# A four-layer diffusion trunk on one core: ten planned orders for its instruction queues, wider products in the last layer, and sixteen softmax scalings on GpSimd

## The chip, the core and the metric

One core of a Trainium2 chip runs the whole program. The metric is the time on the device of one execution, in microseconds (us). The core has TensorE (PE in the rows; its weight loads stand apart as PEld), VectorE (DVE), ScalarE (ACT), GpSimd (POOL) and SyncE (SP), which issues the DMAs. Each engine works through its own queue in order, and the queues wait for each other by semaphores.

## The reference, cut to what matters

Two streams of 256 tokens by 1024 features go through four layers: the latent tokens `x` and the context tokens `ctx`. Each layer has an attention and a SwiGLU feed-forward part, both with a norm before and after. The context reads only itself, the latent stream reads both. After the last layer's keys and values the context isn't needed any more.

```python
for i in range(DEPTH):                      # mixers 0, 1, 2, 0 = A, B, C, A
    h  = rmsnorm(x, g[0]) * (1.0 + sc1) + sh1
    hc = rmsnorm(ctx, g[0]) * (1.0 + csc1) + csh1
    y, yc = attention(h, hc, ...)
    x = x + gt1 * rmsnorm(y, g[1])
    h = rmsnorm(x, g[2]) * (1.0 + sc2) + sh2
    x = x + gt2 * rmsnorm(swiglu(h, ffn_w13[i], ffn_w2[i]), g[3])
    if not last:
        ctx = ...                           # the same, with yc and its own modulation
```

All is fp32. The feed-forward part is `(silu(h @ gate) * (h @ up)) @ w2` with 2816 hidden features.

## The kernel before, in words

**Products.** Every fp32 operand of a large product is split into a high and a low part (`wh`, `wl` of a weight tile, `hh`, `hl` of an activation), and `mm3` (lines 520 to 524) issues three matmuls: high by high, high by low, low by high. Weights come in units of 512 KB: a DMA into `wr`, ACT copies it to `wh` (line 420), DVE subtracts to `wl` (line 536). A unit is 128 output features of `q`, `k`, `gate` or `up` (`feature_major`, weights stationary, 256 tokens of one stream moving), or a piece of `v`, `o`, `w2` (`token_major`, `block_unit_product`, activations stationary, 512 weight columns moving). In the first three layers `gate` and `up` of both streams go together from the third unit on: `feature_major_both` moves 512 columns, the tokens of both streams side by side. That works since `both_h[k]` holds, for feature block k, the high parts of the context and the latent tokens and then the low parts of both, in one tile of four times 256 columns.

**Attention.** For each head, `scores` are matmuls, DVE takes the maximum (or adds bias or mask and takes it in one step), ACT takes the exponential with its sum, the rows are scaled by the reciprocal sum, `flip` transposes the result on TensorE, and a product with `v` follows (`att_a`, `att_bc`). In layer C (the third) the latent queries come in two tiles of 128; the first tile's 128 by 512 exponentials are scaled on DVE (line 1057), the second's on ACT, and the context's, 128 by 256 at a time, on GpSimd (line 1054). GpSimd also does half of the rotary embedding (lines 872, 873) and the two small steps of each norm (704, 706).

**Order.** Nothing is emitted where it is written. Every step is an `Op` with an engine, an assumed duration and a priority; `Plan.schedule` puts all of them in an order by list scheduling, `Plan.latest` goes back through it for latest starts, and the next round mixes both into new priorities (`ROUNDS`). The order with the shortest planned time is emitted. While it picks a step, the scheduler holds a PSUM bank that one engine touched closed to the others until that engine's step has ended (`touch`).

**Seams.** At the end of `o` and of `w2` the residual and both norms have to be gone through (`emit_kept`: ACT squares, DVE, GpSimd, DVE), then TensorE transposes the result (`prenorm_flips`, line 762), and ACT and DVE split it into the operands of the next products. The planner puts the products of one stream over the norm chain of the other.

## Time and profile before

| | |
|---|---|
| median of 3 runs | 2272.24 us (2271.04 to 2272.55) |
| the profiled execution | 2271.76 us |
| its span, first to last instruction | 2269.9 us |
| TensorE busy | 2209.3 us (97%) |
| VectorE busy | 1636.9 us (72%) |
| ScalarE busy | 1061.1 us (47%) |
| GpSimd busy | 218.7 us (10%) |
| mean granted clock of TensorE | 0.992 |

The ends of matmuls are modelled, so that matmuls which follow each other without a pause overlap in the record, and a busy TensorE isn't one at its peak. Read the distance from one start to the next instead: where it is the shortest that this form shows, TensorE is the limit; where it is longer, TensorE waited. The rows that the argument rests on have a section of their own below.

### The profile page before, as it was taken

What the parts mean: (1) busy time and instruction counts of PE and PEld (TensorE: products, weight loads), DVE (VectorE), ACT (ScalarE), POOL (GpSimd) and SP (SyncE); (2) the same over time, 40 slices, a digit from 0 to 9 for tenths busy, and PEclk for the clock granted to TensorE, in tenths of its full rate; (3) what the DMA queues carried; (4) which work ended last, traced back from release to release, by engine and by line L of the source; (5) the groups of instructions that cost most, each with busy time, mean ns of one, the idle gap of its engine ahead of it and who ended that gap; (6) DMA issues with size and microseconds to landing.
All of it is one profiled execution on the core that took longest, in us unless ns stands there. A gap on an engine that the chain in (4) does not pass through costs nothing.

```text
span 2269.9 us, 35835 instructions
## 1 busy us (share of the span) xinstructions
PE 2209.3 (97%) x13236; PEld 1926.1 (85%) x13236; DVE 1636.9 (72%) x3114; ACT 1061.1 (47%) x2245; POOL 218.7 (10%) x300
## 2 busy tenths in 40 slices
PE   7999999999999999999999999999999999998998
PEld 5889888888888998888878899888887878997997
DVE  5888699887354887878773489997877345996454
ACT  5478642223344776522233469852223333785443
POOL 0111010000011231200000032020000000311000
PEclk9999999999999999999999999999999999999999
DMA  9743266664243433566643430256664233444653
GB/s 298 221 122 117 87 200 230 213 209 159 96 121 100 114 100 112 177 206 201 195 145 107 126 93 12 84 185 194 209 193 146 102 112 94 132 119 131 185 185 140
DMA packets 369278, 338.91 MB, mean 149 GB/s; under 512 B 33120, under 2 KB 282960, under 8 KB 369104
## 3 DMA queue, kind: packets, MB, share of 16 engines
q1 hardware_dynamic: 369104, 336.63, 47.2%
q8 instruction: 104, 1.70, 0.3%
q14 instruction: 70, 0.57, 0.1%
HBM read 321.77 MB, written 1.17 MB: 142 GB/s over the span
## 4 chain that ended last, share of the span: by engine, by line
PE 84%; DVE 9%; ACT 3%; issue 2%; POOL 1%; DMA 1%; DVEq 0%; POOLq 0%; SPq 0%; ACTq 0%
PE bkl L522 19%; PE bkl L524 19%; PE bkl L523 19%; PE bkc L523 7%; PE bkc L522 7%; PE bkc L524 6%; ACT f L420 1%; DVE wl L536 1%; PE bkc L650 1%; PE bkl L935 1%; DVE r L943 1%; DVE col L923 1%; DVE r L884 1%; PE bkl L915 1%; PE bkl L762 1%
## 5 line engine op out<-in xcount | busy, mean ns | idle before, releaser
L420 ACT ACTIVATE wh<-wr 128x1024 fp32r<-128x1024 f32 x380 | 402.6, 1061 | 818.7 <-PE bkl L523 502.5
L536 DVE TENSOR_TENSOR wl<-wr,wh 128x1024 fp32r<-128x1024 f32 x380 | 469.5, 1237 | 339.8 <-ACT wh L420 338.5
L522 PE MATMUL bkl<-h,wh 128*128 128x256 f32 (+1 forms) x1872 | 637.3, 340 | 0.0
L524 PE MATMUL bkl<-h,wl 128*128 128x256 f32 (+1 forms) x1872 | 632.0, 338 | 0.0
L523 PE MATMUL bkl<-h,wh 128*128 128x256 f32 (+1 forms) x1872 | 631.9, 338 | 0.0
L643 DVE SCALAR_TENSOR_TENSOR f<-f,cs,f 128x512 f32<-128x512 f32 x556 | 386.6, 745 | 7.2 <-DMA f<-in_ada_w 6.5
L522 PEld LDWEIGHTS bkl<-h,wh 128*128 128x128 f32 x1872 | 355.5, 190 | 42.4 <-issue 4.5
L524 PEld LDWEIGHTS bkl<-h,wl 128*128 128x128 f32 x1872 | 355.3, 190 | 37.9
L523 PEld LDWEIGHTS bkl<-h,wh 128*128 128x128 f32 x1872 | 355.5, 190 | 36.9
L522 PE MATMUL bkl<-wh,h 128*128 128x512 f32 (+1 forms) x560 | 219.5, 392 | 0.0
L524 PE MATMUL bkl<-wh,h 128*128 128x512 f32 (+1 forms) x560 | 216.6, 387 | 0.0
L523 PE MATMUL bkl<-wl,h 128*128 128x512 f32 (+1 forms) x560 | 216.5, 387 | 0.0
L522 PE MATMUL bkc<-wh,h 128*128 128x512 f32 (+1 forms) x472 | 185.4, 393 | 0.0
L523 PE MATMUL bkc<-wl,h 128*128 128x512 f32 (+1 forms) x472 | 183.3, 388 | 0.5 <-DVE wl L536 0.5
L524 PE MATMUL bkc<-wh,h 128*128 128x512 f32 (+1 forms) x472 | 183.1, 388 | 0.6 <-DVE h L716 0.6
L704 POOL TENSOR_SCALAR col<-col 128x1 f32<-128x1 f32 x58 | 33.5, 578 | 1485.5 <-ACT j L420 1422.9
L523 PE MATMUL bkc<-h,wh 128*128 128x256 f32 x496 | 142.2, 287 | 2.4 <-DVE h L776 2.3
L522 PE MATMUL bkc<-h,wh 128*128 128x256 f32 x496 | 143.2, 289 | 0.8 <-ACT h L420 0.8
L524 PE MATMUL bkc<-h,wl 128*128 128x256 f32 x496 | 141.5, 285 | 0.0
L522 PEld LDWEIGHTS bkl<-wh,h 128*128 128x128 f32 x560 | 105.3, 188 | 22.0 <-issue 1.0
L524 PEld LDWEIGHTS bkl<-wh,h 128*128 128x128 f32 x560 | 105.2, 188 | 21.6
L523 PEld LDWEIGHTS bkl<-wl,h 128*128 128x128 f32 x560 | 105.3, 188 | 19.9
(215 smaller groups left out, 3395.5 us busy)
## 6 DMA issues: line engine op xcount, KB each, us to landing
wr<-in_ffn_w SPq DMA_DIRECT2D x264, 512.0 KB, 3.9
f<-in_ada_w SPq DMA_DIRECT2D x384, 256.0 KB, 4.4
wr<-in_a_wqkv SPq DMA_DIRECT2D x48, 512.0 KB, 3.8
f<-gd SPq DMA_DIRECT2D x54, 256.0 KB, 5.2
r<-r SPq DMA_DIRECT2D x96, 128.0 KB, 2.3
wr<-in_b_wqkv SPq DMA_DIRECT2D x24, 512.0 KB, 3.8
wr<-in_a_wo SPq DMA_DIRECT2D x16, 512.0 KB, 3.5
wr<-in_c_wqkv SPq DMA_DIRECT2D x12, 512.0 KB, 3.8
```

Of the source, the lines that this page charges most:

```text
L420: nc.scalar.activation(o(), i(), func, **k)
L522: nc.tensor.matmul(o, lh, rh, start=first, stop=False)
L523: nc.tensor.matmul(o, lh, rl, start=False, stop=False)
L524: nc.tensor.matmul(o, ll, rh, start=False, stop=last)
L536: dve(lambda: nc.vector.tensor_tensor(l.ap, raw.ap, f32(h.ap[:]), ALU.subtract), t_dve(1024), [raw, h], [l], p)
L643: dve(lambda b=b, raw=raw, c=c: nc.vector.scalar_tensor_tensor(b.ap, raw.ap, c(), b.ap, ALU.mult, ALU.add), t_dve(512, extra=0.06), [raw, ...
L650: nc.tensor.matmul(acc.ap[32 * j:32 * j + 32, u * 256:(u + 1) * 256], lhs, tiles[j // 2].ap[:, (j % 2) * 256:(j % 2 + 1) * 256], start=fir ...
L704: op("pool", 0.25, lambda: nc.gpsimd.tensor_scalar(r.ap[:, 1:2], ss.ap[:, 0:1], ss.ap[:, 1:2], D * EPS, ALU.add, ALU.add), [ss], [r])
L762: nc.tensor.transpose(tp.ap[:, c0:c0 + P], xn[t, k // 4].ap[:, (k % 4) * P:(k % 4 + 1) * P], ident.ap)
L884: dve(lambda r0=r0, r1=r1, m=m: nc.vector.scalar_tensor_tensor(qs.ap[r1, m, :], src()[r0], QSCALE, f32(qs.ap[r0, m, :]), ALU.mult, ALU.sub ...
L915: nc.tensor.matmul(o, q, kt()[:, 0, :], start=True, stop=False)
L923: dve(lambda: nc.vector.tensor_reduce(nm.ap[:, 0:n], b.ap[:].rearrange("p (i k) -> p i k", i=n), AX.X, ALU.max, negate=True), t_dve(512), ...
```

## The change

**The planner.** Ten rounds in place of four; each tuple now has two entries more (`hold`, `shake`; `shake` is zero in all ten). The `touch` rule goes out of the scheduler. In its place each finished order is gone through once more by a new function, `replay`, with other durations for some steps and with waits between the engines on a bank, and the order whose replayed time is the shortest is emitted. With `hold`, DVE and ACT may leave a step for a more urgent one that is ready within 0.4 of the step's duration.

**The last layer.** `k` of both streams is one product of 512 columns (`QK_BOTH = (3,)`). The latent stream's `gate` and `up` go through `feature_major_parts`: for each feature block one matmul of 512 columns with `wh` (the latent tokens' high parts and, beside them, their low parts), and one of 256 columns with `wl`. The two halves of the bank are two partial sums, and `sum_parts` adds them: ACT copies one half to SBUF, DVE adds the other. For this the latent low parts are put where the context's low parts were (`hlc`).

**GpSimd.** In layer C the first latent query tile's scaling moves from DVE's `tensor_scalar` to a GpSimd `tensor_tensor` whose second operand is the reciprocal, broadcast along the row.

```diff
-ROUNDS = [(0.0, 0.0), (0.7, 0.05), (0.7, 0.05), (0.75, 0.0)]
+ROUNDS = [(0.0, 0.0, 0.0, 0.0), (0.7, 0.05, 0.0, 0.0), (0.7, 0.05, 0.0, 0.0), (0.75, 0.05, 0.0, 0.0), (0.6, 0.05, 0.0, 0.0),
...
-QK_BOTH = False
+QK_BOTH = (3,)
+ON_POOL = {"B": [], "C": [0]}
...
-            time = max(o.end for o in order)
+            time = self.replay(order)
...
+    def replay(self, order):
+        free, end, held, users, bank = {}, {}, {}, {}, {}
+        for o in order:
...
+            t = free.get(o.eng, 0.0)
+            for x in o.deps:
+                t = max(t, end[x] + (0.0 if x.eng == o.eng else AFTER[x.eng]))
...
+        return max(end[o] for o in order)
...
-                    for b in o.bufs:
-                        if b.touch:
-                            for other, end in b.touch.items():
-                                if other != e:
-                                    t = max(t, end + LAT)
...
+                    if self.hold and e in ("dve", "act"):
+                        sooner = [x for x in can if t < x[0] < t + self.hold * o.dur and x[1] < p - URGENT]
+                        if sooner:
+                            t, p, q, o = min(sooner)
...
+                if i == DEPTH - 1 and which == 1:
+                    lb = Buf(f"hlc{k}")
...
+    def feature_major_parts(s, w, H, bank):
+        wh, wl, h3, l3 = w
+        for half in range(2):
+            def go(half=half):
+                for k in range(4 * half, 4 * half + 4):
+                    parts = both_h[k][:].rearrange("p m s t -> p (m s t)")[:, T:3 * T]
+                    wide = bank.ap[:]
+                    if k < KD - 1:
+                        nc.tensor.matmul(wide, h3()[:, k, :], parts, start=(k == 0), stop=False)
+                    nc.tensor.matmul(bank.ap[:, 0:T], l3()[:, k, :], both_h[k][:, 0, 1, :], start=False, stop=False)
+                    if k == KD - 1:
+                        nc.tensor.matmul(wide, h3()[:, k, :], parts, start=False, stop=True)
+            pe(4 * 0.325, go, [wh, wl] + [b for k in range(4 * half, 4 * half + 4) for b in H[k]], [bank], unit=True)
+
+    def sum_parts(bank):
+        x, y = Buf("f1"), Buf("f1")
+        act(lambda: x.ap, lambda: bank.ap[:, T:2 * T], AF.Copy, t_act(T), [bank], [x])
+        dve(lambda: nc.vector.tensor_tensor(y.ap, bank.ap[:, 0:T], x.ap, ALU.add), t_dve(T), [bank, x], [y])
+        return y
...
+                    elif qts[0] in ON_POOL[kind] and j >= FROM[kind]:
+                        op("pool", 1.35, lambda e=e, r=r: nc.gpsimd.tensor_tensor(
+                            e.ap, e.ap, r.ap[:, 0:1].to_broadcast([P, nk]), ALU.mult), [r], [e])
...
+            if last:
+                gate_bank = Buf("bk" + s, cap=("gu" + s, 4))
+                feature_major_parts(s, w, S.H, gate_bank)
+                boost[0] = BOOST["F"]
+                g, S.sg = sum_parts(gate_bank), Buf("f1")
+                act(lambda sg=S.sg: sg.ap, lambda: g.ap, AF.Silu, t_act(T, False), [g], [S.sg])
...
-            if both and unit[0] in "qk" and QK_BOTH:
+            if both and unit[0] in "qk" and L in QK_BOTH:
```

What the planner makes of it, at three places. Names: `bkc` and `bkl` are PSUM banks of the context and the latent stream, `h_72` to `h_79` the tiles `both_h[0]` to `both_h[7]`, `ident` the identity of a transpose, `f_...` a buffer of 128 by 512 or 128 by 256 elements. Lines 522 to 524 are 561 to 563 in the changed file, 762 is 801, 872 and 873 are 936 and 937, 1054 is 1118.

TensorE, the seam from `o` to the feed-forward part in layer A, first layer: before, the last latent products of `o` and then the transposes of the context's norm.

```order
L522 MATMUL bkl<-wh,h_79 128x512
L523 MATMUL bkl<-wl,h_79 128x512
L524 MATMUL bkl<-wh,h_79 128x512
L762 MATMUL bkc<-ident,f_3729 128x128
L762 MATMUL bkc<-ident,f_3757 128x128
```

The same seam in the changed program, between the first and the second pair of transposes.

```order
L801 MATMUL bkc<-ident,f_3685 128x128
L801 MATMUL bkc<-ident,f_3700 128x128
L561 MATMUL bkl<-wh,h_76 128x512
L562 MATMUL bkl<-wl,h_76 128x512
L563 MATMUL bkl<-wh,h_76 128x512
L561 MATMUL bkl<-wh,h_77 128x512
L562 MATMUL bkl<-wl,h_77 128x512
L563 MATMUL bkl<-wh,h_77 128x512
L561 MATMUL bkl<-wh,h_78 128x512
L562 MATMUL bkl<-wl,h_78 128x512
L563 MATMUL bkl<-wh,h_78 128x512
```

Before, all latent products stand ahead of all context transposes; now 12 latent products of 512 columns stand between the two pairs of transposes and 6 behind the second, ahead of the first context `gate`.

TensorE, the seam from the third layer to the fourth: before, from the last context product of `w2` on (18 latent products of 512 columns, lines 522 to 524 in turn, up to the two rows of transposes at the end).

```order
L524 MATMUL bkc<-wh,h_77 128x512
L522 MATMUL bkl<-wh,h_75 128x512
L523 MATMUL bkl<-wl,h_75 128x512
L524 MATMUL bkl<-wh,h_75 128x512
L522 MATMUL bkl<-wh,h_75 128x512
```

The same place in the changed program.

```order
L563 MATMUL bkc<-wh,h_77 128x512
L561 MATMUL bkl<-wh,h_74 128x512
L562 MATMUL bkl<-wl,h_74 128x512
L563 MATMUL bkl<-wh,h_74 128x512
L561 MATMUL bkl<-wh,h_74 128x512
```

Six products more, those of `h_74`, now stand behind the last context product: 24 in place of 18 ahead of the first transpose of the context's norm.

GpSimd in layer C, the middle of the heads: before, the rotary steps of the latent stream (872, 873) and the context's scalings (1054).

```order
L1054 TENSOR_TENSOR f_14208<-f_14208,col 128x256 x2
L1054 TENSOR_TENSOR f_14215<-f_14215,col 128x256 x2
L872 TENSOR_TENSOR f_14399<-f_14399,sinT 128x256
L873 TENSOR_TENSOR f_14519<-f_14519,f_14399 128x256
L1054 TENSOR_TENSOR f_14385<-f_14385,col 128x256 x2
```

In the changed program, with the latent scalings (1121) between them.

```order
L936 TENSOR_TENSOR f_14275<-f_14275,sinT 128x256
L937 TENSOR_TENSOR f_14218<-f_14218,f_14275 128x256
L1121 TENSOR_TENSOR f_14226<-f_14226,col 128x512
L1118 TENSOR_TENSOR f_14320<-f_14320,col 128x256 x2
L1118 TENSOR_TENSOR f_14331<-f_14331,col 128x256 x2
L936 TENSOR_TENSOR f_14480<-f_14480,sinT 128x256
L1121 TENSOR_TENSOR f_14270<-f_14270,col 128x512
L937 TENSOR_TENSOR f_14493<-f_14493,f_14480 128x256
```

Sixteen instructions of 128 by 512 elements stand newly in GpSimd's queue, ahead of context scalings and even between the two steps of one rotary embedding.

## Rows read from the trace of the kernel before

**Rows 1.** The page's first part: busy time of an engine, its share of the span, number of instructions.

```profile
PE 2209.3 (97%) x13236; PEld 1926.1 (85%) x13236; DVE 1636.9 (72%) x3114; ACT 1061.1 (47%) x2245; POOL 218.7 (10%) x300
```

**Rows 2.** Busy time by stretch: the stretch and its length, then for each engine the busy us and the instructions that began, then the granted clock of TensorE, the DMA share and GB/s. In turn: the end of the first layer's attention, its seam, the second layer's seam, the third layer's attention, its seam, the pause before the fourth layer, the transposes and first products after it, the fourth layer's attention, its `gate` and `up`.

```profile
170.00:293.00 123.00, 120.92 (x830) 106.96 (x829) 94.57 (x206) 86.74 (x221) 19.91 (x26) 1.00 0.37 112
293.00:304.00 11.00, 7.77 (x49) 6.81 (x49) 11.00 (x21) 8.45 (x23) 4.35 (x7) 0.84 0.49 172
...
925.00:934.00 9.00, 6.93 (x42) 6.40 (x41) 9.00 (x17) 8.15 (x19) 4.28 (x5) 0.81 0.90 289
...
1300.00:1480.00 180.00, 172.34 (x1312) 163.57 (x1311) 162.63 (x471) 146.67 (x415) 43.90 (x59) 1.00 0.23 68
1480.00:1512.00 32.00, 30.81 (x193) 27.06 (x192) 29.44 (x50) 21.84 (x51) 11.17 (x16) 1.00 0.66 208
...
1869.00:1874.00 5.00, 0.46 (x5) 0.14 (x2) 4.10 (x6) 4.63 (x13) 2.92 (x4) 0.80 0.16 38
1874.00:1882.30 8.30, 7.54 (x23) 6.09 (x24) 7.90 (x14) 3.52 (x10) 2.35 (x5) 0.50 0.37 114
...
1925.00:2060.00 135.00, 128.94 (x964) 122.33 (x963) 119.12 (x249) 97.47 (x219) 30.05 (x32) 0.99 0.45 129
...
2077.00:2206.00 129.00, 129.00 (x1065) 128.43 (x1064) 63.67 (x74) 56.68 (x76) 0.00 (x0) 1.00 0.59 176
```

**Rows 3.** The timeline of TensorE at full clock: start, duration, engine, line, operation, tiles, form. The first two rows are the first and the last of 32 matmuls of 512 columns that follow each other without a pause; the last five, from the fourth layer's start, are matmuls in a row, one of 512 columns and then four of 256.

```profile
1861.82 0.39 PE L523 MATMUL bkl<-wl,h 128*128 128x512 f32 x1
...
1868.85 0.39 PE L524 MATMUL bkl<-wh,h 128*128 128x512 f32 x1
...
1925.36 0.39 PE L524 MATMUL bkl<-wh,h 128*128 128x512 f32 x1
...
1925.58 0.28 PE L522 MATMUL bkl<-h,wh 128*128 128x256 f32 x1
...
1925.70 0.28 PE L523 MATMUL bkl<-h,wh 128*128 128x256 f32 x1
...
1925.82 0.28 PE L524 MATMUL bkl<-h,wl 128*128 128x256 f32 x1
...
1925.94 0.28 PE L522 MATMUL bkl<-h,wh 128*128 128x256 f32 x1
```

**Rows 4.** Groups of instructions of the last layer's `gate` and `up` (2076 to 2207 us): line, engine, operation, tiles, form, count, then busy us and mean ns of one, then idle time before them.

```profile
L523 PE MATMUL bkl<-h,wh 128*128 128x256 f32 x352 | 99.9, 284 | 0.0
...
L420 ACT ACTIVATE wh<-wr 128x1024 fp32r<-128x1024 f32 x45 | 47.6, 1058 | 72.7 <-PE bkl L523 72.3 <-PE bkl L524 0.3
L420 ACT ACTIVATE f<-bkl 128x256 f32<-128x256 f32 x22 | 8.1, 368 | 0.0
...
L536 DVE TENSOR_TENSOR wl<-wr,wh 128x1024 fp32r<-128x1024 f32 x45 | 55.2, 1226 | 64.9 <-ACT wh L420 64.9
L1410 DVE TENSOR_TENSOR gal<-bkl,f 128x256 f32<-128x256 f32 x16 | 6.7, 419 | 0.5 <-ACT f L420 0.5
```

**Rows 5.** The timeline of TensorE at the seams of the first, the second and the third layer; in brackets the engine's idle time before the instruction and what ended it.

```profile
297.31 0.98 PE L762 MATMUL bkc<-ident,f 128*128 128x128 f32 x7 [2.92 <-DVE f L745]
...
927.05 0.39 PE L522 MATMUL bkc<-h,wh 128*128 128x256 f32 x1 [0.78 <-ACT h L420]
...
928.72 0.38 PE L523 MATMUL bkc<-h,wh 128*128 128x256 f32 x1 [1.29 <-DVE h L776]
...
1874.00 1.97 PE L762 MATMUL bkc<-ident,f 128*128 128x128 f32 x8 [4.54 <-DVE f L745]
...
1876.72 0.90 PE L762 MATMUL bkc<-ident,f 128*128 128x128 f32 x3 [0.76 <-DVE f L745]
```

**Rows 6.** Stretches in which TensorE's granted clock stood at half, behind the idle times of rows 5 (columns as in rows 2), and the timeline of matmuls of 256 and of 512 columns inside them.

```profile
298.50:301.90 3.40, 3.36 (x15) 2.98 (x16) 3.40 (x8) 1.63 (x6) 1.01 (x3) 0.50 0.02 8
930.00:933.40 3.40, 3.40 (x18) 3.40 (x17) 3.40 (x6) 3.34 (x6) 1.25 (x1) 0.51 0.87 321
1872.10:1882.20 10.10, 7.45 (x23) 6.00 (x24) 8.80 (x16) 5.08 (x14) 4.08 (x8) 0.50 0.34 98
...
300.16 0.41 PE L522 MATMUL bkc<-h,wh 128*128 128x256 f32 x1
...
300.38 0.41 PE L523 MATMUL bkc<-h,wh 128*128 128x256 f32 x1
...
1878.70 0.63 PE L522 MATMUL bkc<-wh,h 128*128 128x512 f32 x1
...
1879.13 0.63 PE L523 MATMUL bkc<-wl,h 128*128 128x512 f32 x1
```

**Rows 7.** The third layer's attention (1300 to 1480 us): the groups of DVE's and of GpSimd's scalings; line 1054 over the whole execution (minimum, median and maximum ns of one); a GpSimd instruction that ran while DVE split a weight tile; and TensorE's waits for a transpose (`flip`, line 935) in this stage: us in total, times, longest.

```profile
L1057 DVE TENSOR_SCALAR f<-f,col 128x512 f32<-128x512 f32 x16 | 7.9, 499 | 0.1
...
L1054 POOL TENSOR_TENSOR f<-f,col 128x256 f32<-128x256 f32 x32 | 21.1, 682 | 34.0 <-ACT f L420 15.9 <-DVE col L1049 7.4 <-DVE col L1051 5.7
...
L1054 POOL TENSOR_TENSOR f<-f,col x64: 607/615/1595, 732.8 to 1395.7; 128x256 f32<-128x256 f32 x64
...
1334.35 1.22 DVE L536 TENSOR_TENSOR wl<-wr,wh 128x1024 fp32r<-128x1024 f32 x1
1334.43 1.73 POOL L873 TENSOR_TENSOR f<-f,f 128x256 f32<-128x256 f32 x1
...
PE bkl L935 <- ACT f L420: 1.6, 2, 1.4
PE bkl L935 <- DVE f L1057: 1.3, 1, 1.3
...
PE bkl L935 <- DVE col L1051: 0.9, 1, 0.9
```

More of the change, by code (lines that the diff above doesn't have):

```diff
@@ L2 @@
 import math
+import random
 from contextlib import ExitStack
@@ L58 @@
 ALONE = 2
-QK_BOTH = False
+QK_BOTH = (3,)
 LATE = 5
+ON_POOL = {"B": [], "C": [0]}
+FROM = {"B": 0, "C": 0}
+URGENT = 4.0
+SEED = 1
+NEAR = 8.0
+TRUE_PE = [(12 * 0.109, 12 * 0.120), (6 * 0.216, 6 * 0.227), (12 * 0.216, 12 * 0.227), (4 * 0.325, 4 * 0.347),
+           (0.436, 0.472), (0.872, 0.944), (0.654, 0.72), (0.66, 0.5)]
+AFTER = {"pe": 0.2, "act": 0.15, "dve": 0.12, "pool": 0.12, "dma": 0.0}
 TAIL = {"o": 0, "early o": 2, "w2": 4}
@@ L168, in run @@
         self.times = []
-        for mix, wait in ROUNDS:
+        noise = random.Random(SEED)
+        for mix, wait, self.hold, shake in ROUNDS:
             for b, c in count.items():
                 b.left = c
-                b.touch = {}
             for b in self.fixed:
@@ L177, in run @@
                 for o, (start, late) in zip(self.ops, now[1]):
-                    o.prio = (1 - mix) * start + mix * late
+                    o.prio = (1 - mix) * start + mix * late + (noise.uniform(-shake, shake) if shake else 0.0)
             try:
@@ L185, in run @@
                 continue
-            time = max(o.end for o in order)
-            self.times.append(round(time, 1))
+            time = self.replay(order)
+            self.times.append((round(max(o.end for o in order), 1), round(time, 1)))
             if best is None or time < best[0]:
                 best = time, order, [b.slot for b in self.fixed], [(o.start, o.end) for o in self.ops]
-            if now is None or time < now[0] + TOL:
+            if now is None or time < now[0] + TOL and time < best[0] + NEAR:
                 late = self.latest(order)
@@ L206, in run @@
             o.fn()
+    def replay(self, order):
+        free, end, held, users, bank = {}, {}, {}, {}, {}
+        for o in order:
+            d = o.dur
+            if o.eng == "pe":
+                d = next((b for a, b in TRUE_PE if abs(d - a) < 0.001), d)
+            elif o.eng == "pool":
+                d = {0.7: 1.0, 0.25: 0.45, 0.4: 0.6, 0.75: 0.8}.get(d, d)
+            t = free.get(o.eng, 0.0)
+            for x in o.deps:
+                t = max(t, end[x] + (0.0 if x.eng == o.eng else AFTER[x.eng]))
+            for x in o.after:
+                t = max(t, end[x, "start"])
+            for b in o.bufs:
+                if b.slot is not None and b.slot >= 0:
+                    at = self.kinds[b.kind][0], b.slot
+                    if held.get(at) is not b:
+                        users[at, 0] = users.get((at, 1), [])
+                        users[at, 1] = []
+                        held[at] = b
+                    for x in users[at, 0]:
+                        t = max(t, end[x] + (0.0 if x.eng == o.eng else AFTER[x.eng]))
+                    if b.kind[:2] == "bk":
+                        for x in users[at, 1]:
+                            if x.eng != o.eng:
+                                t = max(t, end[x] + 0.1)
+                    users[at, 1].append(o)
+            end[o, "start"] = t
+            free[o.eng] = t + d
+            end[o] = t + d + (2.5 if o.eng == "dma" else 0.0)
+        return max(end[o] for o in order)
     def latest(self, order):
@@ L314, in schedule @@
             cand[o.eng].remove(o)
-            for b in o.bufs:
-                if b.kind[:2] == "bk":
-                    b.touch[o.eng] = o.end
             for b in o.bufs:
@@ L1404, in run_unit @@
         elif nm == "up":
+            dst, at = (S.g[0], n) if n < 16 else (S.g[1], n - 16)
+            if last:
+                up_bank, sg = Buf("bk" + s, cap=("gu" + s, 4)), S.sg
+                feature_major_parts(s, w, S.H, up_bank)
+                boost[0] = BOOST["F"]
+                u = sum_parts(up_bank)
+                dve(lambda: nc.vector.tensor_tensor(dst.ap[:, at, :], u.ap, sg.ap, ALU.mult), t_dve(T), [u, sg], [(dst, at)])
+                boost[0] = 0.0
+                return
             gu, sg = S.gu, Buf("f1")
-            dst, at = (S.g[0], n) if n < 16 else (S.g[1], n - 16)
             feature_major(s, w, S.H, gu, T)
```

6 lines of the change are left out of this document (4 added, 2 removed).

## The prediction

> **What bounds the kernel now.** I read the page's busy times first: TensorE is busy 97% of the span, DVE 72%, GpSimd 10% [rows 1]. TensorE's ends are modelled, so I went to the stretches by stage and to the distances between its starts. At full clock, 31 steps between 32 matmuls of 512 columns take 7.03 us, 0.227 us each; three steps of 256 columns take 0.36 us, 0.120 us each [rows 3]. Two matmuls of 256 columns thus cost 0.240 us, one of 512 costs 0.227 us: 13 ns go with the instruction, not with its columns. By these distances TensorE runs without a gap through the last layer's `gate` and `up` [rows 2]. What it loses elsewhere, it loses in two kinds of place. At the seams between `o` and the feed-forward part, and ahead of the last layer, it stands idle for a norm chain, and behind that its granted clock is at half (1.2 in place of 2.4 GHz) for 3.4 or 10.1 us [rows 5, 6]. In the attention of the third and fourth layers it is busy 172.3 of 180 and 128.9 of 135 us, with DVE close behind at 162.6 and 119.1 us [rows 2]. So an edit pays in full if it saves TensorE's own time in the feed-forward stage, or its idle time at a seam; in attention, only as far as DVE's and GpSimd's chains let it.
>
> **The last layer's gate and up.** There are 44 units of 8 feature blocks, 352 blocks with three matmuls of 256 columns each [rows 4]. Before: 352 x 3 x 0.120 us. After: 352 x (0.227 + 0.120) us. The difference is 352 x 0.013 = 4.6 us, on TensorE's own path in a stage where nothing else ends last. No row shows the two widths in turn on the same bank; the step from 512 to 256 columns takes 0.22 us, and the next ones 0.12 us [rows 3]. The bounds: nothing, if the 13 ns come back in the mixed pair, and 9.2 us, if the weight load behind the wide matmul hides so well that the narrow one loses its 13 ns too. I take -4.6 us, since both distances are this kernel's own. What is added is hidden: 44 ACT copies of 0.37 us, 16 us more on an ACT that is busy 57 of 129 us, and 44 DVE additions of 0.42 us, 18 us more on a DVE busy 64 of 129 us [rows 2, 4]. Were that cover gone, a unit's copy and addition, 0.8 us, would hold one bank longer, and four are allowed for.
>
> The Trainium skill ("TensorE: Matmul & The Clock Gate", under "Wait — 56ns, not 53.3ns?") puts the fixed cost of a warm matmul at 2.5 ns beyond its columns. By it this edit would be worth 352 x 2.5 ns = 0.9 us. The 13 ns in the rows disagree, and the rows decide; the case stands among the rivals.
>
> **The last layer's k.** Eight units, 24 matmuls each for both streams: 192 pairs become 192 wide ones, 192 x 0.013 = 2.5 us of TensorE. The stage has DVE at 119.1 of 135 us and idle places of its own, and now the splits of both streams' keys come at once. I take -2.0 us, between 0 and -2.5.
>
> **The seams.** Four places lose idle time and, behind it, clock. I price the clock by the rows at half: 256 columns take 0.215 us there, so 3.4 us lose 3.4 x (1 - 0.120 / 0.215) = 1.5 us; 512 columns take 0.43 us, so the 8.3 us of TensorE's work between 1874.0 and 1882.3 lose 8.3 x (1 - 0.227 / 0.43) = 3.9 us [rows 2, 6].
> First layer: 2.9 us idle for the second pair of transposes, and 1.5 us of clock: 4.4 us at stake. Before, all latent products of `o` stood ahead of the context's transposes; now 12 of them, 2.7 us, stand between the two pairs and 6 behind. I take -3.5 us.
> Second layer: 0.8 + 1.3 us idle ahead of the first `gate` matmuls [rows 5] and 1.5 us of clock, 3.6 us at stake. The changed order sets the last latent products behind the transposes here as well. I take -2.5 us.
> Third layer: TensorE is busy 30.8 of 32 us [rows 2], 1.2 us at stake. I take -0.8 us.
> Ahead of the fourth layer: 4.5 + 0.8 us idle [rows 5] and 3.9 us of clock. Six more products of 0.227 us, 1.4 us, now stand behind the last context product. The idle time falls to some 3 us, and I leave the clock as it is: -1.4 us, or up to -5.3 if it no longer falls for as long.
> Together -8.2 us. The ends are 0, if the chains through ACT, DVE and GpSimd, which are reordered too, get as much longer, and -14.5 us, the whole stake. The fifth seam, in the last layer, has one stream and nothing to put over it; it stays.
>
> **The scaling on GpSimd.** DVE loses 16 x 0.499 = 8.0 us of the 162.6 us that it works in this stage. GpSimd gets 16 instructions of twice the elements of line 1054, whose median is 0.615 us: up to 16 x 1.23 = 19.7 us, beside 43.9 us of work in 180 us, so it isn't the bound by its total [rows 2, 7]. But each scaling now takes 0.73 us longer ahead of its transpose. And beside a weight split on DVE a step of the rotary embedding took 1.73 us on GpSimd, and line 1054's longest is 1.595 us against its median of 0.615 [rows 7]: about 1 us more where that happens, so 1.7 us longer. Queued behind each are the context's scalings and the rotary steps of the next heads; the latent scores wait for those, with a whole head's products in between. TensorE already waited 3.8 us in this stage for transposes that had late inputs [rows 7]. Those are four waits among 32 latent transposes of scaled tiles, so most have some cover. I take +2 us: three of the sixteen exposed at 0.73 us. The ends are -4 us, if DVE's 8.0 us shorten the waits for DVE, and +27 us, sixteen times 1.7.
>
> The Trainium skill ("GPSIMD Engine Reference", under "8. Key points") speaks against this edit: DVE is about twice as fast for elementwise work, and GpSimd shares its SBUF interfaces with DVE's instructions that read two SBUF tensors. The weight split is such an instruction, and the trace agrees with both: 0.615 us for half the elements that DVE does in 0.499 us, and 1.73 us beside a split [rows 7].
>
> **The rest of the new order** in attention: steps move by a few places on every engine, some waits get more work over them and some less. I see no sign in it: 0, plus or minus 5 us.
>
> **The sum.** -4.6 - 2.0 - 8.2 + 2.0 = -12.8 us. Against the profiled execution's 2271.76 us (span 2269.9 and 1.9 around it), that is 2259.0 us; that execution stands 0.5 us under the median of 2272.24, so the median after is 2259 us, 0.6% less.
>
> **The rivals.** A measurement of this kernel tells 0.2%, 4.5 us, from no change; the border is at 2267.7 us.
> *GpSimd becomes the late engine (slower).* Each of the sixteen transposes waits for its scaling: 16 x 1.2 us, between the free and the contended price, is 19 us in place of 2, so 2259 + 17 = 2276 us. For it: GpSimd works in order, its steps beside weight splits take a microsecond more, and six scalings stand in a row at the end of the stage. Against it: 180 us hold 64 us of GpSimd work, and few flips waited before. It decides from some 1 us of uncovered wait per flip on. 9 in 100.
> *The order gives nothing.* Where one wait goes, another engine's queue is next; the seams come out as before, and what stays are the wider products and GpSimd's price: -4.6 - 2.0 + 2.0, so 2267 us, on the border. For it: the planner's durations are assumed ones, and the new durations are in the choice alone, not in the picking. 15 in 100, half of it within 0.2%.
> *The seams give all.* The idle times go and the clock stays up, -14.5, with the products' -6.6 and nothing for GpSimd: 2251 us. 18 in 100.
> *The wide matmuls save only 2.5 ns each* (the page's rule): 0.9 + 0.5 us in place of 6.6, so 2264 us. Against it stand all the distances of rows 3. 5 in 100.
> My forecast has the other 53 in 100.
>
> **How the numbers follow.** 2259 us is the likeliest case. Its own spread is about 2252 to 2266. The range goes up to 2270, over the case without gain from the order, and down to 2247, under the case in which the seams give all; it leaves out the slower case and little else. Faster by over 0.2%: the forecast's 53, 18, 5, and about half of the 15, less a few for the spread: 78 in 100. Within 0.2%: 13. Slower: 9.
>
> **What would show it.** In the profile after: blocks of the last `gate` and `up` every 0.347 us, and the stage some 5 us shorter; idle times ahead of the context's transposes and the first `gate` under 1 us in the first two layers, with no half clock behind them; under 4 us ahead of the fourth layer. In the third layer's attention, 16 GpSimd steps of 1.2 us and more, DVE 8 us less, and waits for `flip` that name GpSimd of 2 us in all. The prediction is wrong if those waits come to over 10 us, if the seams' idle times stand elsewhere again, or if the mixed pairs of 512 and 256 columns take 0.36 us.

## The result, and the profile after

| | before | after |
|---|---|---|
| median, same chip | 2271.77 us (6 runs, 2270.07 to 2272.67) | 2259.65 us (6 runs, 2258.39 to 2261.73) |
| ratio, 95% interval | | 0.9948 [0.9935, 0.9961] |
| span of the profiled execution | 2269.9 us | 2257.8 us |
| mean granted clock of TensorE | 0.992 | 0.996 |

The changed kernel is 0.52% faster; 2259.0 us were predicted. The page's first part, busy time by engine, answers to [rows 1]:

```profile
PE 2200.0 (97%) x12692; PEld 1892.5 (84%) x12692; DVE 1649.2 (73%) x3142; ACT 1074.6 (48%) x2289; POOL 235.9 (10%) x316
```

TensorE has 544 matmuls (192 of `k`, 352 of `gate` and `up`) and 9 us less. DVE has 12 us more, which the additions bring: e9 below, without GpSimd's scaling, has 12.6 us more too (1649.5 us). That the sixteen scalings went freed next to nothing on DVE, for a reason that e3 shows.

To see where the 12 us are, I cut both traces at the same matmuls, each time at the first of a named unit. "L1" to "L3" is the context's ninth `gate` unit of the first to the third layer.

| stretch, us | before | after | difference |
|---|---|---|---|
| start to L1 | 390.12 | 386.20 | -3.9 |
| L1 to L2 | 630.13 | 630.75 | +0.6 |
| L2 to L3 (holds layer C's attention) | 568.78 | 570.67 | +1.9 |
| L3 to the fourth layer's first `q` | 336.56 | 331.76 | -4.8 |
| to its first `gate` | 149.75 | 147.69 | -2.1 |
| to its first `w2` | 127.45 | 124.42 | -3.0 |
| to the end | 67.08 | 66.34 | -0.7 |

The timeline of TensorE after, at the first layer's seam and ahead of the fourth layer, answers to [rows 5]; the stretches (columns as in rows 2) answer to [rows 2, 6]: the first and the second layer's seam, the third layer's attention, a part of it at half clock, its seam, the two parts of the pause ahead of the fourth layer, the fourth layer's attention, the half clock at its end, its `gate` and `up`.

```profile
288.82 0.39 PE L563 MATMUL bkl<-wh,h 128*128 128x512 f32 x1
289.05 1.03 PE L801 MATMUL bkc<-ident,f 128*128 128x128 f32 x8
289.84 0.48 PE L561 MATMUL bkl<-wh,h 128*128 128x512 f32 x1
...
292.67 1.03 PE L801 MATMUL bkc<-ident,f 128*128 128x128 f32 x8
293.46 0.48 PE L561 MATMUL bkl<-wh,h 128*128 128x512 f32 x1
...
294.92 0.28 PE L561 MATMUL bkc<-h,wh 128*128 128x256 f32 x1
...
1867.78 0.27 PE L801 MATMUL bkc<-ident,f 128*128 128x128 f32 x1
1870.47 1.09 PE L801 MATMUL bkc<-ident,f 128*128 128x128 f32 x8 [2.42 <-DVE f L784]
1872.33 0.55 PE L801 MATMUL bkc<-ident,f 128*128 128x128 f32 x3 [0.77 <-DVE f L784]
```

```profile
289.00:300.00 11.00, 10.94 (x75) 9.91 (x74) 10.94 (x19) 7.70 (x18) 3.17 (x5) 1.00 0.82 246
920.00:929.00 9.00, 8.89 (x60) 7.91 (x58) 8.94 (x16) 6.32 (x15) 2.52 (x4) 1.00 0.79 241
1298.00:1478.00 180.00, 172.45 (x1296) 162.81 (x1295) 161.76 (x452) 145.13 (x409) 57.72 (x74) 0.99 0.22 64
1378.30:1381.60 3.30, 3.30 (x17) 3.30 (x17) 3.30 (x14) 1.72 (x9) 0.00 (x0) 0.50 0.03 12
1478.00:1510.00 32.00, 31.25 (x198) 27.86 (x197) 27.45 (x46) 22.14 (x52) 11.97 (x16) 1.00 0.65 205
1864.00:1869.00 5.00, 4.05 (x19) 3.06 (x18) 5.00 (x7) 4.97 (x13) 1.47 (x2) 1.00 0.08 9
1869.00:1877.00 8.00, 5.63 (x29) 4.09 (x30) 7.34 (x14) 6.15 (x15) 4.29 (x7) 1.00 0.38 132
1919.00:2049.00 130.00, 123.45 (x760) 110.34 (x759) 113.27 (x248) 95.80 (x215) 29.70 (x32) 0.99 0.45 130
2069.00:2191.00 122.00, 122.00 (x694) 106.05 (x693) 75.71 (x107) 65.76 (x111) 0.00 (x0) 1.00 0.61 182
...
2057.50:2067.70 10.20, 4.19 (x18) 3.83 (x19) 8.15 (x13) 6.31 (x16) 4.29 (x6) 0.50 0.35 103
```

At the first seam the transposes now stand between products, with no idle time in brackets and the clock at 1.00; before it was 2.92 us idle and then 3.4 us at half. The second seam looks the same. Ahead of the fourth layer 2.4 + 0.8 us are idle in place of 4.5 + 0.8, and in this profile the clock stays up where it stood at half for 10.1 us. The 10.2 us at half ahead of the last `gate` (2057.5) are the fifth seam, which stayed.

In the third layer's attention the clock fell for 3.4 us (from 1378.2), where before it did not. This is what the +1.9 us of L2 to L3 are. Seven variants below run the same order; in the profiles of three of them (e1b, e8, e11) the clock stays up there, and L2 to L3 takes 568.87 us in each, as long as before (568.78). In the profiles of after, e2 and e5b, with the same steps, it falls once for 3.4 us, and the stretch takes 569.8 to 570.7 us. The same attention in e8:

```profile
1298.00:1478.00 180.00, 172.48 (x1307) 162.81 (x1306) 163.14 (x454) 146.62 (x412) 57.72 (x74) 1.00 0.23 66
```

The mixed pair in the last `gate` and `up` answers to [rows 3]; the first and the last row bound the stage:

```profile
2067.07 0.78 PE L898 MATMUL bkl<-h,wh 128*128 128x512 f32 x1
...
2099.84 0.40 PE L898 MATMUL bkl<-h,wh 128*128 128x512 f32 x1
...
2100.07 0.28 PE L899 MATMUL bkl<-h,wl 128*128 128x256 f32 x1
...
2100.18 0.40 PE L898 MATMUL bkl<-h,wh 128*128 128x512 f32 x1
...
2100.43 0.28 PE L899 MATMUL bkl<-h,wl 128*128 128x256 f32 x1
...
2100.55 0.40 PE L898 MATMUL bkl<-h,wh 128*128 128x512 f32 x1
...
2191.49 0.40 PE L561 MATMUL bkl<-wh,h 128*128 128x512 f32 x1
```

From 2099.84 to 2100.18 it is 0.34 us, from there to 2100.55 it is 0.37: the pairs aren't alike. Over the whole stage (both kinds of distance, leaving out the first pieces at half clock) the wide ones are 0.235 us from the next start, the narrow ones 0.117 us: 0.352 us for a pair, not 0.347.

Layer C's scaling on GpSimd answers to [rows 7]: the group in 1298 to 1480 us, its minimum, median and maximum in ns, and TensorE's waits for a transpose (`flip`, now line 999) in this stage; the last row is a wait of the second layer that before did not have.

```profile
L1121 POOL TENSOR_TENSOR f<-f,col 128x512 f32<-128x512 f32 x16 | 17.4, 1092 | 31.7 <-DVE col L1115 16.7 <-ACT f L459 7.6 <-ACT r L459 6.8
...
L1121 POOL TENSOR_TENSOR f<-f,col x16: 1037/1042/1485, 1367.0 to 1458.1; 128x512 f32<-128x512 f32 x16
...
PE bkl L999 <- DVE col L1089: 1.3, 1, 1.3
PE bkl L999 <- ACT f L459: 0.8, 1, 0.8
PE bkl L999 <- POOL f L1121: 0.2, 1, 0.2
...
PE bkc L647 <- DVE c L656: 1.5, 1, 1.5
```

GpSimd's step takes 1.04 us, and one flip waits for it, 0.2 us.

### The profile page after: what moved, and what is told of

It reads as the page before. It is cut to its first block, busy times and chain, and to the rows that moved or that the text cites. A ratio compares the mean times of both kernels' runs of the same rounds, so it can differ in the third digit from the quotient of the medians.

```text
span 2257.8 us, 34921 instructions
## 1 busy us (share of the span) xinstructions
PE 2200.0 (97%) x12692; PEld 1892.5 (84%) x12692; DVE 1649.2 (73%) x3142; ACT 1074.6 (48%) x2289; POOL 235.9 (10%) x316
## 4 chain that ended last, share of the span: by engine, by line
PE 80%; DVE 9%; ACT 4%; DMA 3%; issue 2%; POOL 2%; SPq 0%; DVEq 0%; POOLq 0%; ACTq 0%
PE bkl L561 17%; PE bkl L562 17%; PE bkl L563 17%; PE bkc L561 6%; PE bkc L563 6%; PE bkc L562 6%; PE bkl L898 3%; PE bkl L899 2%; DVE wl L575 2%; ACT f L459 2%; PE bkl L999 1%; PE bkc L689 1%; ACT r L459 1%; DVE r L1007 1%; POOL col L743 1%
## 5 line engine op out<-in xcount | busy, mean ns | idle before, releaser
L561 PE MATMUL bkl<-h,wh 128*128 128x512 f32 (+1 forms) x1520 | 544.8, 358 | 3.3 <-DVE f L934 1.8
L563 PE MATMUL bkl<-h,wl 128*128 128x512 f32 (+1 forms) x1520 | 539.7, 355 | 0.0
L562 PE MATMUL bkl<-h,wh 128*128 128x512 f32 (+1 forms) x1520 | 539.6, 355 | 0.0
L561 PEld LDWEIGHTS bkl<-h,wh 128*128 128x128 f32 x1520 | 288.0, 189 | 48.3 <-issue 5.0
L563 PEld LDWEIGHTS bkl<-h,wl 128*128 128x128 f32 x1520 | 287.8, 189 | 40.5
L562 PEld LDWEIGHTS bkl<-h,wh 128*128 128x128 f32 x1520 | 288.1, 190 | 39.4
L561 PE MATMUL bkc<-h,wh 128*128 128x256 f32 x432 | 123.6, 286 | 0.0
L562 PE MATMUL bkc<-h,wh 128*128 128x256 f32 x432 | 122.5, 284 | 0.2
L563 PE MATMUL bkc<-h,wl 128*128 128x256 f32 x432 | 122.2, 283 | 0.0
```

The costliest lines, as they stand in the source:

```text
L561: nc.tensor.matmul(o, lh, rh, start=first, stop=False)
L562: nc.tensor.matmul(o, lh, rl, start=False, stop=False)
L563: nc.tensor.matmul(o, ll, rh, start=False, stop=last)
```

## The experiments

The theory: the order pays at the seams, the wider products pay some 5 us in the last layer, and GpSimd's scaling costs nothing. The rivals: the products or the order do all of it; the scaling is what layer C's +1.9 us came from. Seven variants change only how a step is written, and so keep the changed kernel's order step by step (e1b, e2, e3, e4, e5b, e8, e11); the other four are planned anew. Times are medians; ratios are against the kernel before on the same chip.

| run | order | products | scaling on GpSimd | us | ratio |
|---|---|---|---|---|---|
| before | old | no | no | 2271.77 | 1 |
| e9_old_planner_no_scale | old | yes | no | 2265.33 | 0.9970 [0.9959, 0.9980] |
| e7_old_planner | old | yes | yes | 2271.29 | 1.0000 [0.9991, 1.0009] |
| e6_planner_alone | new | no | no | 2265.97 | 0.9980 [0.9971, 0.9989] |
| e10_new_planner_no_scale | new | yes | no | 2264.06 | 0.9965 [0.9952, 0.9977] |
| after | new | yes | yes | 2259.65 | 0.9948 [0.9935, 0.9961] |
| e3_scale_on_dve | that of after | yes | no, same place | 2262.33 | 0.9962 [0.9948, 0.9976] |
| e12_four_rounds | new, 4 rounds | yes | yes | 2274.80 | 1.0015 [1.0006, 1.0024] |

### The parts and the planner

**e6_planner_alone.** `QK_BOTH = ()`, `ON_POOL` empty, `feature_major` for the last `gate` and `up`.

> The new planner (ten rounds, replay, no ready time of banks) plans the kernel before: no mixed products in gate and up, the last layer's k for each stream alone, no scaling on GpSimd. If the seams' loss came from the order alone, the first two layers' seams are without half clock here too and the whole is 2264 to 2267 us (before minus 5 to 8). Rival: the rounds happen on a good order only with the new products in, the half clock stands at some seams, and the whole is within 2 us of before (2270 to 2274 us).

2265.97 us, as the theory had it. Its trace has no half clock at the first two seams, and ahead of the fourth layer it stays up too: L3 to the first `q` takes 329.4 us, 7 us less than before. But there is 3.4 us at half at 168.5 us, in the first layer's attention, and start to L1 takes 390.0 us, as long as before. L2 to L3 takes 570.5 us without any scaling on GpSimd, with two stretches of 3.4 us at half (at 1404 and 1448 us): in this order, too, the clock can fall in layer C's attention.

**e7_old_planner.** The scheduler and the four rounds of before, with all else of the change.

> The planner of before (four rounds, the best by the planner's own end) plans the changed kernel's work: the mixed products, k over both streams and GpSimd's scaling are in. By the parts (2.1 us of gate and up, 2.5 us of k, nothing of GpSimd) the whole is 2266 to 2269 us, with the seams of the first two layers again at half clock. Rival: the order gives nothing by itself, the products and the scaling give all, and the whole is that of the changed kernel, 2258 to 2261 us.

2271.29 us: neither. The last layer gained (`q` to `gate` 145.7 us, to `w2` 124.8 us: 6.7 us less than before), but L2 to L3 took 576.4 us, 7.6 us more. The place is layer C's seam: the timeline of TensorE and of DVE there, then the stretch behind it.

```profile
1500.53 1.41 DVE L844 SCALAR_TENSOR_TENSOR x_l<-f,col,x_l 128x512 f32<-128x512 f32 x2
...
1502.39 1.41 DVE L844 SCALAR_TENSOR_TENSOR x_l<-f,col,x_l 128x512 f32<-128x512 f32 x2 [0.45 <-POOL col L716]
...
1503.72 0.48 DVE L788 SCALAR_TENSOR_TENSOR h<-bkc,mod,h 128x256 fp32r<-128x256 f32 x1
...
1504.25 0.58 PE L533 MATMUL bkc<-h,wh 128*128 128x256 f32 x1 [3.62 <-DVE h L788]
...
1503.50:1510.30 6.80, 5.82 (x26) 5.44 (x27) 6.80 (x16) 4.19 (x12) 1.89 (x4) 0.50 0.59 214
```

In the kernel before, DVE does the first of these splits (there L776) ahead of the latent residual (there L832):

```profile
1495.87 1.41 DVE L776 SCALAR_TENSOR_TENSOR h<-bkc,mod,h 128x256 fp32r<-128x256 f32 x3
1497.20 0.74 DVE L832 SCALAR_TENSOR_TENSOR x_l<-f,col,x_l 128x512 f32<-128x512 f32 x1
```

In e7 DVE's queue holds four passes of the latent residual (L844) ahead of the split (L788) that the context's first `gate` needs. TensorE stands idle for 3.62 us, and then the clock is at half for 6.8 us. No GpSimd scaling is near: what the scaling changed is the plan.

**e9_old_planner_no_scale.** `ON_POOL = {"B": [], "C": []}` on top of e7.

> The planner of before with the mixed products and k over both streams, and without GpSimd's scaling (layer C's first tile on VectorE as before). With the scaling in, the old planner's kernel gained 6.7 us in the last layer and lost 7.6 us in layer C. If the scaling is what cost the old order those 7.6 us, layer C (first layer C gate 8 after the second layer's) is back at 569 us and the whole is 2264 to 2266 us. Rival: the planner's order of layer C changes for the worse with any change of the steps behind it, and the whole stays at 2269 to 2272 us.

2265.33 us: the first theory. L2 to L3 is back at 569.0 us, `q` to `gate` is 145.4 us and to `w2` 125.1 us. So the products by themselves are worth 0.3% in the old order.

**e10_new_planner_no_scale.** The same line on top of the changed kernel.

> The changed kernel without GpSimd's scaling, planned anew: VectorE scales layer C's first tile, wherever the new planner then puts it. If GpSimd's scaling is worth what it gave at an equal order (2.3 us in layer C), the whole is 2261 to 2263 us. Rival: the new planner finds an order that does without it at no loss, 2257 to 2260 us, and the scaling is worth nothing.

2264.06 us, a little above the first theory's 2261 to 2263. Its interval overlaps that of the changed kernel by little. L2 to L3 takes 569.2 us, no more than after; its loss is in start to L1, 390.5 us against 386.2: in the first layer's attention TensorE waits 2.95 us for a DMA (`r<-r`), and 6.8 us of half clock follow, from 167 us on. Again the step's presence changed the plan far from the step.

**e12_four_rounds.** `ROUNDS` cut to its first four tuples.

> The changed kernel, planned by the new planner in its first four rounds alone: it then takes the third round's order, whose planned end by replay is 6.5 us behind that of the seventh, which the ten rounds choose. If the rounds beyond the fourth are what gave the order its gain, the whole is 2264 to 2268 us. If the gain lies in what all new rounds share (a bank's last use by another engine no longer delays its next planned use), the first two layers' seams are without half clock and the whole is 2258 to 2262 us.

2274.80 us: neither, and slower than before. The first two seams show no half clock here too, so what all new rounds share does give that. But L1 to L2 takes 635.2, L2 to L3 574.4, and the fourth layer's `q` to `gate` 153.0 us, with 6.8 us at half at 2022 us: 4.4, 3.7 and 5.3 us more than in the changed kernel. In the last of these stretches TensorE's longest waits, other than that of the fifth seam:

```profile
PE bkl L561 <- DVE r L1006: 4.7, 4, 2.7
PE bkl L560 <- ACT r L458: 2.6, 2, 1.8
```

These are the products of the softmax weights with `v`; they wait for the two parts (`r`) into which ACT and DVE split the transposed weights (L1006 is in `flip`). The ten rounds chose another order, which is worth 15 us, more than all edits of the products and the scaling.

### The scaling, at an unchanged order

**e3_scale_on_dve.**

```diff
-nc.gpsimd.tensor_tensor(e.ap, e.ap, r.ap[:, 0:1].to_broadcast([P, nk]), ALU.mult)
+nc.vector.tensor_scalar(e.ap, e.ap, r.ap[:, 0:1], None, ALU.mult)
```

The 16 instructions go into DVE's queue at the same places.

> The scaling of layer C's first latent query tile goes back to VectorE (tensor_scalar by the column), at the very place in the order where GpSimd's stands; all else stays. If the move to GpSimd is a help there (VectorE has 16 x 0.5 us less to do in a stage where matmuls wait for it), layer C's stretch from the second layer's last w2 to layer C's first gate gets 1 to 4 us longer and the whole 2261 to 2264 us. If the move is the cost that shows as 3 us more stall in layer C's attention, the stretch gets 2 to 3 us shorter and the whole 2257 us.

2262.33 us, L2 to L3 572.0 us. The six profiles with the changed kernel's own steps in that stretch (after, e1b, e2, e5b, e8, e11) have 568.9 to 570.7 us. So by the time the scaling on GpSimd is rather a help, of 1 to 3 us; the two intervals overlap, so its size isn't settled. Most of the difference in the stretch is clock: in e3's profile it falls twice there for 3.4 us, in the others once or not at all. Whether the scaling on DVE brings on the second fall isn't shown.

What the edit does to DVE is plain. Its busy time over the whole execution is 1650.5 us in e3, and 1648.7 to 1650.6 us in the six profiles that scale on GpSimd in the same order. The 16 scalings take 0.48 us each in e3, 7.7 us in all, so taking them off DVE freed less than 2 us of it: its other steps get longer while GpSimd scales. The clearest are 32 additions of one column in layer C's attention, first in the kernel before, then in e3, in the changed kernel and in e4 below (us busy, mean ns); last, the same line in the changed kernel with its minimum, median and maximum in ns:

```profile
L1049 DVE TENSOR_TENSOR col<-col 128x1 f32<-128x1 f32 x32 | 4.2, 155 | 0.2
L1113 DVE TENSOR_TENSOR col<-col 128x1 f32<-128x1 f32 x32 | 4.7, 159 | 0.1
L1113 DVE TENSOR_TENSOR col<-col 128x1 f32<-128x1 f32 x32 | 8.2, 267 | 0.1
L1113 DVE TENSOR_TENSOR col<-col 128x1 f32<-128x1 f32 x32 | 10.7, 345 | 0.1
L1113 DVE TENSOR_TENSOR col<-col x48: 127/152/994, 1322.2 to 1471.8; 128x1 f32<-128x1 f32 x32, 128x2 f32<-128x2 f32 x16
```

The more 128 by 512 passes GpSimd makes (none, 16, 32), the longer the same additions take; in the changed kernel the eight that such a pass overlaps have a mean of 0.60 us, the 21 that no GpSimd instruction overlaps 0.145 us.

**e4_scale_twice.**

```diff
+nc.gpsimd.tensor_tensor(e.ap, e.ap, ones.ap[:, 0:1].to_broadcast([P, nk]), ALU.mult)
 nc.gpsimd.tensor_tensor(e.ap, e.ap, r.ap[:, 0:1].to_broadcast([P, nk]), ALU.mult)
```

> Ahead of each of the 16 scalings GpSimd makes one more pass over the same tile (a product with ones), so that the scaled tile comes some 1.04 us later; the order stays. If GpSimd lies off the path (waits that name its scaling hold 0.6 us in all), the whole grows by 0 to 4 us, 2260 to 2264 us. If the tile's delay is on the path, as a part of the 3 us more stall in layer C's attention, it grows by most of 16 x 1.04 = 17 us, 2272 to 2277 us.

2267.58 us (2263.65 to 2271.46, ratio 0.9986 [0.9977, 0.9995]): between the two. In the stage, first the added and the scaling pass, then TensorE's wait that names it, and two waits that grew:

```profile
L1121 POOL TENSOR_TENSOR f<-f,ones 128x512 f32<-128x512 f32 x16 | 19.3, 1209 | 9.1 <-ACT f L459 9.1
...
L1122 POOL TENSOR_TENSOR f<-f,col 128x512 f32<-128x512 f32 x16 | 17.3, 1081 | 13.4 <-DVE col L1115 10.5 <-DVE col L1096 2.3
...
PE bkl L999 <- POOL f L1122: 1.2, 2, 0.9
PE bkl L1136 <- DVE col L1089: 1.8, 1, 1.8
PE bkc L979 <- DVE r L948: 1.6, 1, 1.6
```

Some 17 us more of GpSimd (252.8 us busy against 235.9) made the kernel 8 us longer, of which L2 to L3 (575.5 us) has 5 to 6.6 us. TensorE's waits in this stretch add up to 12.8 us in place of 7.6; only 1.2 us carry GpSimd's name, and most of the rest names DVE, whose 32 additions above are the longest here. So the first microsecond was covered, and of a second one about half isn't.

### The products

**e1b_narrow_gate_up.** Each wide matmul of `gate` and `up` in two:

```diff
-nc.tensor.matmul(wide, h3()[:, k, :], parts, start=(k == 0), stop=False)
+nc.tensor.matmul(wide[:, 0:T], h3()[:, k, :], parts[:, 0:T], start=(k == 0), stop=False)
+nc.tensor.matmul(wide[:, T:2 * T], h3()[:, k, :], parts[:, T:2 * T], start=False, stop=False)
```

> Each 512-column matmul of the last layer's gate and up becomes two of 256 columns into the same two halves of the bank; the order of the work and all else stay. If the pair of a 512-column and a 256-column matmul costs 0.354 us as its spacing in the changed kernel says, and three of 256 columns cost 3 x 0.120 = 0.360 us, the stretch from the first gate block to the first w2 block (124.4 us in the changed kernel) becomes 124.4 + 352 x 0.006 = 126.5 us, and the whole 2262 us. Rival A (the pair saves the predicted 0.013 us, and a part of it is lost elsewhere in the stretch): 129 us. Rival B (wide and narrow matmuls have nearly the same fixed cost, 352 x 0.0025): 125.3 us.

2264.48 us (0.9965 [0.9952, 0.9979]); the stage takes 128.11 us. This lies between the theory's 126.5 and rival A's 129 us. Its distances are 0.120 us, all of them. 1.0 us of the 3.7 is the half clock of the fifth seam, which in this profile reaches 3.0 us into the stage and in that of the changed kernel 0.6 us. What is left, 2.7 us, is 352 x (0.360 - 0.352) = 2.8 us.

**e2_grouped.** In each half block the four wide matmuls first and then the four narrow ones (the last wide one at the end of the bank's group stays last).

> In each half block of the last layer's gate and up the four 512-column matmuls stand in a row, and behind them the four of 256 columns, in place of one and one alternating; nothing else moves. If it is the alternation of widths that makes the pair 0.354 us, the wide matmuls are spaced 0.227 and the narrow ones 0.120 us again save at the two changes of width of a half block: a pair near 0.349 us, the stretch near 124.4 - 352 x 0.005 = 122.7 us, the whole near 2258 us. If a 512-column operand that spans the high parts of one stream and the low parts of the other or the like is what costs, the wide spacing stays at 0.236 and the stretch at 124.4 us.

2260.19 us (0.9947 [0.9933, 0.9961]), the same as after; the stage takes 124.46 us, of which the half clock takes 1.0 us more than after. The distances are 0.232 and 0.118 us, a pair 0.3495: about half of the 5 ns came back, 0.9 us of 2260, which the time can't show.

**e8_offset.** `[:, 0:2 * T]` in place of `[:, T:3 * T]`: the wide matmuls read the context's and the latent tokens' high parts.

> The 512-column matmuls of the last layer's gate and up read columns 0 to 511 of the four parts (the context's high half beside the latent's high half) in place of 256 to 767 (the latent's high half beside the context's low half or as the parts lie): gate and up of the last layer are computed from other numbers. If where the operand begins costs the 9 ns, the wide spacing falls from 0.236 to 0.227 us and the stretch from the first gate block to the first w2 block from 124.4 to 121.2 us; if it is the alternation of widths, or the operand's form, nothing moves (within 0.5 us).

2259.28 us in one run; the distances are 0.235 and 0.117 us as after (stage 125.32 us, 0.9 us more at half clock). Where the operand begins doesn't matter.

**e11_all_wide.** The narrow matmul reads `parts` and writes `wide`, so it adds the low weights' product with the low parts, which the others leave out.

> The 256-column matmul with the low weights, in the last layer's gate and up, reads the same 512 columns as its neighbour, so that every matmul there is 512 columns wide (the bank's upper half gets one product more, low weights with low parts, and the stretch is longer). If the neighbourhood of two widths is what makes the wide ones 0.235 us apart, all are 0.227 us apart here and the stretch is 704 x 0.227 = 159.8 us. If this operand or this stage is slower, they stay at 0.233 to 0.236 us and the stretch is 164 to 166 us.

2296.42 us in one run. The stage takes 160.1 us, and every distance is 0.227 us (timeline of TensorE):

```profile
2100.03 0.39 PE L898 MATMUL bkl<-h,wh 128*128 128x512 f32 x1
2100.26 0.39 PE L899 MATMUL bkl<-h,wl 128*128 128x512 f32 x1
2100.48 0.39 PE L898 MATMUL bkl<-h,wh 128*128 128x512 f32 x1
```

The first theory: same weights, same banks, same stage, and without the second width the 8 ns are gone. The mixture of widths costs them. (With the width, the part of the bank that is written became the same for all; the two aren't told apart.)

**e5b_narrow_k.** `mm3` over two halves of 256 columns for the last layer's `k`.

> The last layer's k products over both streams are done as two of 256 columns each in the same bank, in the same place of the order. If a 512-column matmul saves 0.120 x 2 - 0.227 = 0.013 us, 192 of them take 2.5 us more: the time from the last layer's first q to its first gate (147.7 us in the changed kernel) becomes 150 us and the whole 2262 us. Rival (the products there end behind other engines, so that their length is hidden): 147.7 us, the whole 2260 us.

2261.88 us (0.9956 [0.9943, 0.9970]), `q` to `gate` 148.2 us. The five profiles with wide products and the same steps there have 146.5 to 147.7 us. That is 0.5 to 1.7 us, of 2.5 us at most; by the time alone it isn't separated from after. The 0.5 us is the fairer figure: in e5b, after and e11 the clock falls for 3.4 us at the same place (1969 to 1970 us), and the last two have 147.7 us; in e1b, e2 and e8, with 146.5 us, it falls at 2010 to 2014 us instead. Added up from start to start, the stage's products of `q` and `k` take 2.3 us more in e5b than in the changed kernel. So most of what the wider `k` saves on TensorE is lost again in attention.

## Why the prediction was right, point by point

The time came out as forecast, 2259.65 us against 2259.0, but not by the forecast's terms: two of them were off by more than 3 us, in opposite ways.

**Gate and up of the last layer (-4.6): right in kind, too large.** The step that failed is "both distances are this kernel's own", put together from matmuls of one width in a row. Side by side the pair takes 0.352 us, so 2.8 us; the stretch has -3.0. e11 shows that it is the mixture, e8 that it is not where the operand begins, e2 that grouping gives back half. What in TensorE makes the pair longer stays open. The rival by which the wide matmuls save only 2.5 ns each fell: one width in a row has 13 ns, and in the mixture 8 are left. The cover over the copies and additions held: TensorE stays at 122.0 of 122 us with ACT at 65.8 and DVE at 75.7.

**The last layer's k (-2.0): the number by luck.** The stretch from `q` to `gate` has -2.1, but undoing k alone, at the same order and with the clock's fall at the same place, gives 0.5 us back (e5b). The step that failed is that k's 2.5 us of TensorE's time would nearly all arrive in a stage with idle places of its own; the rest of the -2.1 belongs to what stands around it. In the old order (e9) that stretch got 4.4 us shorter, and there the clock doesn't fall in it, as it did before at 2025.6 us.

**The seams (-8.2): the mechanism was right, two sizes were not.** First layer: -3.5 forecast, -3.9 in its stretch, and the idle time and the half clock are gone. (In the eight profiles with the changed kernel's order this stretch has 386.0 to 388.8 us, so -1.3 to -4.1; what varies lies ahead of the seam.) Second layer: -2.5 forecast; the idle time and the half clock there are gone, but its stretch has +0.6. A new wait of 1.5 us ahead of a transpose of the modulation vectors (line 647), and some more in attention (its scores' products take 1.5 us longer), gave it back. Third layer and GpSimd together: +1.2 forecast (-0.8 and +2.0), +1.9 measured, of which the half clock in attention is 1.8: without it the stretch has +0.1. Ahead of the fourth layer: -1.4 forecast with -5.3 as the bound, -4.8 measured. The step that failed is "I leave the clock as it is": with 2.4 us idle in place of 4.5, the clock fell for 3.4 us or not at all, in place of 10.1. In the profile of after it did not fall; in all seven others with the same order it stood at half for 3.4 us. That made next to no difference: L3 to the first `q` takes 331.8 us in after and 331.8 to 332.6 in the seven. In e5b the half clock falls on the transposes, and TensorE's second wait there, 0.77 us in after, is gone in return. The fifth seam stayed, as said (10.2 us at half before and after).

**GpSimd (+2.0): too large, within the bounds.** Two steps failed. One is "three of the sixteen exposed at 0.73 us": the instruction takes 1.04 us, not 1.23, beside 0.499 us on DVE, and one flip waits 0.2 us for it. The Trainium skill ("GPSIMD Engine Reference", "8. Key points") calls DVE about twice as fast for elementwise work; this trace agrees. The other is "DVE loses 16 x 0.499 = 8.0 us" and its sign, "DVE 8 us less": in 180 us of that attention DVE is busy 161.8 us in place of 162.6, and at an equal order it has under 2 us less over the whole execution (e3), since its other steps get longer beside GpSimd's. The prediction priced that meeting on GpSimd's side alone. By the time, at an equal order, GpSimd is 1 to 3 us better than DVE (e3), with intervals that overlap. The slower rival, sixteen late transposes, fell. e4 shows that it had a point, only one microsecond further on: another pass on each tile costs 8 us.

**The rest of the order (0, plus or minus 5): the weakest step.** How good the changed kernel's order is hangs on which round it came from: four rounds give 2274.8 us, and without the scaling, which lies in layer C, the ten lose 4.3 us in the first layer (e10, one profile).

**The sum.** By stretches, measured less forecast: gate and up +1.6, k -0.1, first layer -0.4, second +3.1, third with GpSimd +0.7, ahead of the fourth -3.4, the end -0.7 (not forecast): +0.8 in all, -12.0 against -12.8. So the time agrees partly by luck: the second layer and the place ahead of the fourth were off in opposite ways. "The order gives nothing" fell with e6 (0.9980 by the planner alone) and with the gap between e9 and after; "the seams give all" (2251 us) fell by the time, since attention took a part back.

## What to carry to other kernels

Before you credit an edit that a planner reacts to, run it once at an unchanged order and once planned anew: here the same scaling cost 6.0 us in the old plan (e9 to e7), through a seam that it doesn't touch, and gained 4.4 us in the new one (e10 to after, intervals that overlap a little). At a seam, put independent products between the pairs of transposes; here that took the idle time and, behind it, the half clock. Before you give a stretch's 2 us to an edit, look whether the clock fell there in this one execution; another profile of the same order tells. Work that leaves DVE for GpSimd isn't time that leaves DVE: look for the steps that got longer. Price a mixture of matmul widths from a mixture: distances from rows of one width were 5 ns a pair too good.

## What the runs showed of the hardware that was not expected

- Matmuls of 512 columns take 0.227 us in a row, 0.235 us with ones of 256 columns between them, 0.232 us in groups of four; those of 256 columns take 0.120 us in a row and 0.117 us between wide ones.
- A GpSimd product of 128 x 512 fp32 with a broadcast column takes 1.04 us (128 x 256 takes 0.615 us), so the wider form is cheaper per element.
- DVE's steps get longer while GpSimd works: at one and the same order 32 additions of one column take 4.7 us without GpSimd's scalings beside them, 8.2 us with 16 and 10.7 us with 32 passes of 128 x 512 (the longest 0.99 us, the median 0.15 us).
- With one and the same order, the granted clock ahead of the fourth layer fell for 3.4 us in seven profiles and not in the eighth, that of after (2.42 us idle), and the stretch was as long; behind 4.54 us idle, in the kernel before, it fell for 10.1 us.
- In layer C's attention, behind one and the same wait of 1.5 us of TensorE, the clock fell for 3.4 us in the profile of after and not in that of e8; there it cost 1.8 us.
